# Attention blocks of a hybrid transformer step: transposes, values and scores issued in one run ahead of the block's whole filling work

## The chip, the cores and the metric

The kernel runs on one core of a Trainium2 chip. TensorE (PE) does the matrix products and the transposes and writes only into PSUM, whose eight banks hold 512 columns each here. VectorE (DVE), ScalarE (ACT) and GpSimd (POOL) do the elementwise work; the SyncE queue (SP) issues the transfers. The metric is the device time of one execution in microseconds (us).

## The reference

Two trunk layers over 512 latent and 128 context tokens of width 1024. Cut to what matters here:

```python
h = modulate(rms_norm(x, lw['g_attn']), sh1, sc1)
cb, cc, cv, gq, gk, gv, nq, nk, nv, mq, mkv, mkr, gates = in_project(h, lw['w_in'])
y_conv = short_conv(cb, cc, cv, lw['w_conv'])
y_gqa = banded_window_attention(q_g, k_g, v_g, k_ctx, v_ctx, sink, ATTN_SCALE)      # 8 heads
y_na = neighbourhood_attention(nq, nk, nv, k_ctx, v_ctx, lw['na_rpb'], ATTN_SCALE)  # 4 heads
y_mla = dense_attention(q_mla, [k_lat, k_ctx], [v_lat, v_ctx], MLA_SCALE)           # 4 heads, latent keys
out = merge_branches(gates, y_conv, y_gqa, y_na, y_mla, lw)                         # sigmoid gates, then w_o
x = x + gt1 * out
x = x + gt2 * squared_relu_mlp(modulate(rms_norm(x, lw['g_mlp']), sh2, sc2), lw['w_ff1'], lw['w_ff2'])
```

Context tokens go through the same layers with dense attention among themselves. All data is float32.

## The kernel before, in words

**Products.** A float32 product is made of three products of rounded halves, x and w each being split into a high and a low part. `steps` issues, for one half of the tokens (320 columns) and each of eight slices of the inner dimension, three matmuls (lines 226 to 228) into one PSUM bank and then yields, telling 410 ns as its cost; eight such steps fill a bank. These rows are called dense below, three to a step.

**The attention stage** (`mixers`, once a layer) walks 16 heads: 8 windowed, 4 neighbourhood, 4 with latent keys (`Mla`, heads m0 to m3). A head has five blocks of 128 queries: four latent ones, in two pairs, and one of context tokens. So 80 blocks a layer are worked off by `attend`, whose round i handles two of them at once:

- of block i: `block_T` transposes its probabilities on PE (line 568, up to four per bank), ACT copies the high part out of PSUM (line 571), and `block_lo` on DVE makes the low part (line 575), after which the bank is free;
- of block i+3 (AHEAD is 3): `block_scores` (PE lines 503 to 508, into one of two double banks, then the row minimum on DVE), `block_exp` (ACT, line 548), `block_norm` (POOL, line 553);
- of a finished pair: `values_out`, which is `pair_pv` (PE, line 585, probabilities times values), a copy on ACT (line 589) and the sum into y on DVE (lines 598 to 608).

**The fill.** The layer's projections, convolutions and gates are the other half of the stage. They are generators in one list, FILL: `q1` to `q3`, `c0` to `c3`, `nq`, `nk`, `nv`, `ckv`, `mq`, `kr` and `m0` to `m3`, where None is one gate chunk (16 dense steps) and the number of an entry says how many gate chunks are mixed in between its own steps. `fill(ns)` advances them in the order of the list until their costs have used up ns; a task that waits for a head (`wait`) stops the list for that round. RATE is the ns that a block gets. `block_scores` of a head's first block calls `need`, which runs the list up to the tasks of that head at once, whatever it costs, and takes the cost off the next rounds. `m0` to `m3` (`Mla.prep`) project the queries and keys of one latent head (and at m0 and m2 the values of two).

**Order before.** PE's order is the program's. In a round: transposes, half of the block's fill, scores and exp, the other half (PART is 0.5). The product with the values is put off: inside `steps`, after the third step of a fresh bank (FRESH is 2), or after the exp of a round more than one later.

**Banks.** The stage has four single banks, for transposes, values and fill together, and two double banks for scores. DVE, ACT, POOL and SP are put in order by the compiler's scheduler in this stage.

Of the kernel before, what the change touches and what calls it, by code (L numbers as in the profile page):

```python
# [38 lines left out]
GQ, GK, GV, NQC, NK, NV, MQ, MKV, CONV, MKR = 0, 4, 5, 6, 8, 10, 12, 14, 15, 99  # L39
HEAD, GATE = 100, 200  # L40
# [9 lines left out]
_N0, _KV = [("nk0", (NK,), 0), ("nv0", (NV,), 0)], ("ckv", (MKV,), 0)  # L50
_NQ0, _NQ1, _NK1, _NV1 = ("nq0", (NQC,), 0), ("nq1", (NQC + 1,), 0), ("nk1", (NK + 1,), 0), ("nv1", (NV + 1,), 0)
_MQ, _KR = ("mq", (MQ, MQ + 1), 0), ("kr", (MKR,), 0)
_END = [("m0", (HEAD,), 2), None, ("m1", (HEAD + 1,), 1), ("c1", (CONV + 3,), 0), ("m2", (HEAD + 2,), 2),
        ("c2", (CONV + 5,), 0), ("m3", (HEAD + 3,), 1), ("c3", (CONV + 1,), 0), None]
FILL = ([*_Q, _C0, _Q3, None, _NQ0, *_N0, None, _KV, _NQ1, None, _NK1, _MQ, _NV1, None, _KR, *_END],
        [*_Q, None, _C0, _Q3, None, _NQ0, None, *_N0, None, _KV, None, _NQ1, None, None, _NK1, _MQ, _NV1, None, _KR,
         *_END])
# [2 lines left out]
Y_OF = {0: 0, 1: 2, 2: 6, 3: 8}  # L60
OUT_K, OUT_V = 0, 3

RATE = (3400, 3500)
PREP = (820, 600, 1200)


AHEAD, PART, LAG, FRESH = 3, 0.5, 1, 2

OWN, ROOT, SPREAD = 1, 2, 3
COLS = dict(bmod=0, gattn=48, gmlp=56, wconv=64, sink=70, gq=78, gkv=80, gfin=81, n=89)  # L70
# [10 lines left out]
class Net:  # L81
# [137 lines left out]
    def steps(self, out, w, x, sl, ks=None):  # L219

        nc = self.nc
        (whi, wlo), (xhi, xlo) = w, x
        ks = ks or [(k, k) for k in range(KC)]
        n = len(ks)
        for i, (kw, kx) in enumerate(ks):
            nc.tensor.matmul(out, lhsT=whi[:, kw, :], rhs=xhi[:, kx, sl], start=(i == 0), stop=False)  # L226
            nc.tensor.matmul(out, lhsT=whi[:, kw, :], rhs=xlo[:, kx, sl], start=False, stop=False)  # L227
            nc.tensor.matmul(out, lhsT=wlo[:, kw, :], rhs=xhi[:, kx, sl], start=False, stop=(i == n - 1))  # L228
            if i == FRESH:
                self.values_out()  # L230
            yield 410

    def half(self, w, x, h, ks=None):
# [375 lines left out]

    def values_out(self):  # L610


        if self.pv:
            R, self.pv = self.pv[0], None
            self.pair_pv(R)
            self.pair_out(R)
# [23 lines left out]
    def attend(self, blocks, fill, budget):  # L640

        n = len(blocks)
        for i in range(AHEAD):
            self.block_scores(blocks[i])
            self.block_exp(blocks[i])
            self.block_norm(blocks[i])
            fill(budget(blocks[i]))
        for i in range(n + 1):
            self.round = i
            B = blocks[i] if i < n else None  # L650
            A = blocks[i + AHEAD] if i + AHEAD < n else None
            ns = budget(B or blocks[-1])
            if B:
                self.block_T(B)
            self.drain_pe(one=True)
            fill(ns * PART)
            if A:
                self.block_scores(A)
            if B:
                self.block_lo(B)  # L660
            if A:
                self.block_exp(A)
            if self.pv and self.pv[1] < i:
                self.values_out()
            fill(ns * (1 - PART))
            if A:
                self.block_norm(A)
            self.drain(1300)
            if B and (B["u"] == 1 or B["kind"] == "ctx"):
                self.values_out()  # L670
                self.pv = B["pair"], i + LAG
        self.values_out()

# [11 lines left out]
    def mixers(self, l, first):  # L685
# [6 lines left out]
        with ExitStack() as s:  # L692
# [149 lines left out]
            blocks = [b for H in heads for b in self.blocks(H)]  # L842
            rate = lambda B: RATE[l] * (0.45 if B["kind"] == "ctx" else 1)
            self.attend(blocks, fill, rate)
# [784 lines left out]
```

## Time and profile before

| what | value |
|---|---|
| median of 3 runs | 2368.55 us (2368.54 to 2372.35) |
| the profiled execution | 2371.4 us, of which 2369.6 us from its first to its last instruction |
| PE busy | 2302.6 us, 97% of the span |
| DVE, ACT, POOL busy | 1391.4, 935.3, 418.9 us (59%, 39%, 18%) |
| mean granted clock of PE | 0.991 of full speed |

A busy share of PE says how much of the time some matmul was under way; idle time of the other engines costs nothing by itself. A wait in the profile is the idle time of an engine ahead of an instruction, put down to whatever released that instruction last.

### The profile page before, as it was taken

How to read it: one execution, taken by the hardware profiler on the slowest of the kernel's cores; microseconds unless marked ns; L12 is line 12 of the kernel's file. 1: busy time of each engine (PE TensorE's matmuls, PEld its weight loads, DVE VectorE, ACT ScalarE, POOL GpSimd, SP SyncE). 2: the span in 40 equal slices, each digit the busy share in tenths (PEclk: the TensorE clock that was granted, in tenths of full speed). 3: DMA queues.
4: the chain of work that ended last, by engine and by line, in shares of the span. 5: the costliest groups of instructions: out<-in, count | busy, mean ns of one | idle time of the engine just before them, and what ended most of it. 6: DMA issues, size and time to landing. Idle time of an engine off the chain costs nothing. (4 is left out here: it accounts for less than half of the span.)

```text
span 2369.6 us, 39989 instructions
## 1 busy us (share of the span) xinstructions
PE 2302.6 (97%) x15766; PEld 2245.0 (95%) x15766; DVE 1391.4 (59%) x2812; ACT 935.3 (39%) x1971; POOL 418.9 (18%) x496
## 2 busy tenths in 40 slices
PE   8999999999999999999999999999999999999998
PEld 4998998899999999999999999988999999999998
DVE  5766666557765786877566656655434554343433
ACT  5555555432224332222254555554322344131311
POOL 0333333112231000000123333322113200000001
PEclk9999999999999999999999999999999999999999
DMA  6331321155541344444331323211424312222222
GB/s 241 99 104 63 104 87 66 66 202 167 174 154 61 139 162 151 160 144 159 116 135 66 110 89 103 86 66 56 170 94 134 99 54 72 80 72 78 74 81 72
DMA packets 91371, 261.33 MB, mean 110 GB/s; under 512 B 10416, under 2 KB 29232, under 8 KB 89776
## 3 DMA queue, kind: packets, MB, share of 16 engines
q1 hardware_dynamic: 91184, 258.78, 32.5%
q8 instruction: 124, 2.03, 0.3%
q14 instruction: 63, 0.52, 0.1%
HBM read 231.31 MB, written 21.92 MB: 107 GB/s over the span
## 5 line engine op out<-in xcount | busy, mean ns | idle before, releaser
L226 PE MATMUL pr<-hhi,whiw 128*128 128x320 f32 (+1 forms) x2752 | 867.8, 315 | 12.8 <-DVE y L598 3.0
L228 PE MATMUL pr<-hhi,wlow 128*128 128x320 f32 (+1 forms) x2752 | 852.2, 310 | 3.0 <-DVE wlow L193 2.1
L227 PE MATMUL pr<-hlo,whiw 128*128 128x320 f32 (+1 forms) x2752 | 852.7, 310 | 0.1
L226 PEld LDWEIGHTS pr<-hhi,whiw 128*128 128x128 f32 (+1 forms) x2752 | 516.2, 188 | 18.5 <-issue 5.6
L228 PEld LDWEIGHTS pr<-hhi,wlow 128*128 128x128 f32 (+1 forms) x2752 | 515.2, 187 | 5.8 <-DVE wlow L193 3.5
L227 PEld LDWEIGHTS pr<-hlo,whiw 128*128 128x128 f32 (+1 forms) x2752 | 516.1, 188 | 3.7 <-DVE hlo L1255 2.6
L192 ACT CAST whiw<-raww 128x1024 fp32r<-128x1024 f32 (+2 forms) x170 | 173.5, 1021 | 298.4 <-PE pr L227 269.4
L226 PE MATMUL pr<-hh,whiw 128*128 128x320 f32 x832 | 257.1, 309 | 0.0
L227 PE MATMUL pr<-hl,whiw 128*128 128x320 f32 x832 | 256.9, 309 | 0.0
L228 PE MATMUL pr<-hh,wlow 128*128 128x320 f32 x832 | 256.9, 309 | 0.0
L193 DVE TENSOR_TENSOR wlow<-raww,whiw 128x1024 fp32r<-128x1024 f32 (+2 forms) x170 | 208.2, 1225 | 61.5 <-ACT whiw L192 60.8
L1210 POOL TENSOR_TENSOR sqs<-sqs,sq 128x320 f32<-128x320 f32 x48 | 47.7, 993 | 972.1 <-ACT sq L1208 944.4
L1008 DVE SCALAR_TENSOR_TENSOR x<-pr,mod,x 128x256 f32<-128x256 f32 x320 | 107.7, 379 | 188.8 <-PE pr L228 186.5
L553 POOL TENSOR_SCALAR p<-p,sm 128x512 f32<-128x512 f32 (+3 forms) x160 | 120.9, 756 | 400.2 <-DVE sm L552 357.7
L548 ACT ACTIVATE p<-S,sm 128x641 f32<-128x641 f32 (+6 forms) x160 | 112.1, 701 | 156.8 <-DVE sm L539 80.0
L981 POOL TENSOR_TENSOR acc<-acc,sg 128x320 f32<-128x320 f32 x96 | 100.3, 1060 | 339.3 <-DVE sg L980 339.3
L226 PEld LDWEIGHTS pr<-hh,whiw 128*128 128x128 f32 x832 | 156.4, 188 | 0.0
L227 PEld LDWEIGHTS pr<-hl,whiw 128*128 128x128 f32 x832 | 156.4, 188 | 0.0
L228 PEld LDWEIGHTS pr<-hh,wlow 128*128 128x128 f32 x832 | 156.4, 188 | 0.0
L575 DVE TENSOR_TENSOR pt<-pr,pt 128x512 fp32r<-128x512 f32 (+2 forms) x240 | 118.8, 516 | 54.2 <-ACT pt L571 52.9
L276 DVE SCALAR_TENSOR_TENSOR junk<-wm,cb 128x1024 bf16<-128x1024 f32 x112 | 136.8, 1222 | 2.0
L190 POOL TENSOR_TENSOR wlow<-raww,whiw 128x512 fp32r<-128x512 f32 (+1 forms) x72 | 94.7, 1316 | 190.9 <-ACT whiw L189 179.3
(224 smaller groups left out, 3796.2 us busy)
## 6 DMA issues: line engine op xcount, KB each, us to landing
raww<-in_w SPq DMA_DIRECT2D x128, 512.0 KB, 3.6
wm<-in_wm SPq DMA_DIRECT2D x80, 512.0 KB, 3.5
raww<-in_wg SPq DMA_DIRECT2D x64, 512.0 KB, 3.6
raww<-in_wa SPq DMA_DIRECT2D x42, 512.0 KB, 3.6
gdram<-gt SPq DMA_DIRECT2D x28, 320.0 KB, 2.2
wm<-in_wm SPq DMA_DIRECT2D x8, 1024.0 KB, 14.4
raww<-in_wo SPq DMA_DIRECT2D x16, 512.0 KB, 3.5
kt<-kt SPq DMA_DIRECT2D x24, 224.0 KB, 4.8
```

Source lines behind the costliest of these rows:

```text
L190: e.tensor_tensor(lo[:, c], raw[:, c], _r(hi[:, c]), ALU.subtract)
L192: nc.scalar.copy(hi, raw)
L193: nc.vector.tensor_tensor(lo, raw, _r(hi), ALU.subtract)
L226: nc.tensor.matmul(out, lhsT=whi[:, kw, :], rhs=xhi[:, kx, sl], start=(i == 0), stop=False)
L227: nc.tensor.matmul(out, lhsT=whi[:, kw, :], rhs=xlo[:, kx, sl], start=False, stop=False)
L228: nc.tensor.matmul(out, lhsT=wlo[:, kw, :], rhs=xhi[:, kx, sl], start=False, stop=(i == n - 1))
L276: nc.vector.scalar_tensor_tensor(self.junk, raw, 1.0, self.cb[v], ALU.mult, ALU.mult, accum_out=self.mod[l]["mod"][:, v, i:i + 1])
L548: nc.scalar.activation(p[:, :B["n"]], B["sc"], AF.Exp, bias=sm[:, 0:1], scale=-1.0, accum_out=sm[:, 1:2])
L553: nc.gpsimd.tensor_scalar(p[:, :n], p[:, :n], sm[:, 1:2], 1.0, ALU.mult, ALU.mult)
L575: self.nc.vector.tensor_tensor(lo, src, _r(hi), ALU.subtract)
L981: nc.gpsimd.tensor_tensor(a, a, sg, ALU.add)
L1008: self.nc.vector.scalar_tensor_tensor(x[:, j, o + a:o + b], ps[:, a:b], m[:, v, g0 + j:g0 + j + 1], x[:, j, o + a:o + b], ALU.mult, ALU.add)
```

## The change

Three edits. The round of `attend` is rearranged: transposes of block i, then at once the product with the values of the pair that ended in the round before, then the scores of block i+3; the step of the delayed PE work (`drain_pe`) comes after them, and the whole fill of the block behind that, in one piece. `steps` no longer calls `values_out`. RATE goes from 3400 and 3500 to 3600 and 3700. The end of the fill list has a gate chunk ahead of m0, takes one gate chunk each out of m0 and m2, and has one more at the end.

```diff
-_END = [("m0", (HEAD,), 2), None, ("m1", (HEAD + 1,), 1), ("c1", (CONV + 3,), 0), ("m2", (HEAD + 2,), 2),
-        ("c2", (CONV + 5,), 0), ("m3", (HEAD + 3,), 1), ("c3", (CONV + 1,), 0), None]
+_END = [None, ("m0", (HEAD,), 1), None, ("m1", (HEAD + 1,), 1), ("c1", (CONV + 3,), 0), ("m2", (HEAD + 2,), 1),
+        ("c2", (CONV + 5,), 0), ("m3", (HEAD + 3,), 1), ("c3", (CONV + 1,), 0), None, None]
...
-RATE = (3400, 3500)
+RATE = (3600, 3700)
...
-AHEAD, PART, LAG, FRESH = 3, 0.5, 1, 2
+AHEAD, LAG = 3, 1
...
             nc.tensor.matmul(out, lhsT=wlo[:, kw, :], rhs=xhi[:, kx, sl], start=False, stop=(i == n - 1))
-            if i == FRESH:
-                self.values_out()
             yield 410
...
             if B:
                 self.block_T(B)
-            self.drain_pe(one=True)
-            fill(ns * PART)
+            if self.pv and self.pv[1] <= i:
+                self.values_out()
             if A:
                 self.block_scores(A)
             if B:
                 self.block_lo(B)
             if A:
                 self.block_exp(A)
-            if self.pv and self.pv[1] < i:
-                self.values_out()
-            fill(ns * (1 - PART))
+            self.drain_pe(one=True)
+            fill(ns)
             if A:
                 self.block_norm(A)
             self.drain(1300)
             if B and (B["u"] == 1 or B["kind"] == "ctx"):
-                self.values_out()
+                assert self.pv is None
                 self.pv = B["pair"], i + LAG
```

What moves on PE, at three places. The first is a filled round of the first layer, the third block of the first head. Before, three dense matmuls stand between the transposes (line 568) and the values (line 585), and nine more dense ones follow these rows ahead of the scores:

```order
L568 MATMUL pr_1000<-ident_94,p_835 128x128 x4
L568 MATMUL pr_1006<-ident_94,p_835 128x128
L226 MATMUL pr_986<-hhi_89,whiw_863 128x320
L227 MATMUL pr_986<-hlo_90,whiw_863 128x320
L228 MATMUL pr_986<-hhi_89,wlow_864 128x320
L585 MATMUL pr_1012<-pt_875,vt_688 128x256 x8
L585 MATMUL pr_1012<-pt_875,vt_688 128x128 x2
```

Now transposes (line 565), values (line 582) and scores (lines 500 and 501) follow one another:

```order
L565 MATMUL pr_1006<-ident_94,p_838 128x128 x4
L565 MATMUL pr_1012<-ident_94,p_838 128x128
L582 MATMUL pr_1015<-pt_881,vt_688 128x256 x8
L582 MATMUL pr_1015<-pt_881,vt_688 128x128 x2
L500 MATMUL S2_1029<-kt_600,qt_620 128x256
L501 MATMUL S2_1029<-kt_601,qt_620 128x256
L500 MATMUL S2_1029<-kt_600,qt_620 128x256
L501 MATMUL S2_1029<-kt_601,qt_620 128x256
```

The dense rows between them have gone behind the scores.

The second place is the last latent head (m3) of the first layer: the keys of the head are made by lines 1458 to 1460, `kt_5000` and `kt_5001` being what the scores of its first block read. Before, three dense matmuls lie between the making of the keys and their use:

```order
L1458 MATMUL pr_5105<-kt_2397,whib_4781 64x384
L1459 MATMUL pr_5105<-kt_2398,whib_4781 64x384
L1460 MATMUL pr_5105<-kt_2397,wlob_4782 64x384
L226 MATMUL pr_5120<-hhi_89,whiw_5012 128x320
L227 MATMUL pr_5120<-hlo_90,whiw_5012 128x320
L228 MATMUL pr_5120<-hhi_89,wlow_5013 128x320
L506 MATMUL S2_5133<-kt_5000,qt_4998 128x512
L507 MATMUL S2_5133<-kt_5000,qt_4999 128x512
L508 MATMUL S2_5133<-kt_5001,qt_4998 128x512
```

Now the keys (lines 1453 to 1455) are followed by six dense matmuls and a round of the head before, whose scores read `kt_4442`; the first scores of m3 come behind the last of these rows, after 27 dense matmuls and the next round's transposes and values:

```order
L1454 MATMUL pr_4992<-kt_2326,whib_4668 64x384
L1455 MATMUL pr_4992<-kt_2325,wlob_4669 64x384
...
L565 MATMUL pr_5020<-ident_94,p_4858 128x128 x4
L565 MATMUL pr_5026<-ident_94,p_4858 128x128 x2
L503 MATMUL S2_5030<-kt_4442,qt_4440 128x128
L504 MATMUL S2_5030<-kt_4442,qt_4441 128x128
L505 MATMUL S2_5030<-kt_4443,qt_4440 128x128
```

The third place is the end of the first layer's attention stage. Before, nine dense matmuls stand between the last transpose and the last 14 matmuls with the values (of the last pair and of the context block). Now the last ten instructions of the stage have no dense one among them; the row of line 225 is the next stage's first:

```order
L565 MATMUL pr_5376<-ident_94,p_5240 128x128 x4
L565 MATMUL pr_5382<-ident_94,p_5240 128x128 x2
L582 MATMUL pr_5386<-pt_5256,vt_4635 128x256 x12
L565 MATMUL pr_5404<-ident_94,p_5285 128x128 x4
L565 MATMUL pr_5410<-ident_94,p_5285 128x128 x2
L565 MATMUL pr_5417<-ident_94,p_5348 128x128
L582 MATMUL pr_5420<-pt_5375,vt_4635 128x256 x12
L582 MATMUL pr_5437<-pt_5416,vt_4635 128x128 x2
L225 MATMUL pr_5486<-hhi_89,whiw_5289 128x320
```

Counted over the stage by the order of PE's rows, rounds that hold no dense matmul and none of `prep` are: outside the latent heads 11 before and 12 now in the first layer, 3 before and 5 now in the second; in the latent heads (one just ahead of them taken in) 5 and 7 before, and now only the last two rounds of each layer. The number of PE's instructions is the same.

## Rows read from the trace of the kernel before

**Rows 1.** The page: its first lines, span and PE's busy time.

```profile
span 2369.6 us, 39989 instructions
PE 2302.6 (97%) x15766; PEld 2245.0 (95%) x15766; DVE 1391.4 (59%) x2812; ACT 935.3 (39%) x1971; POOL 418.9 (18%) x496
```

**Rows 2.** Busy time by stretch, both attention stages; last columns granted clock, DMA.

```profile
76.00:180.00 104.00, 102.27 (x734) 100.73 (x734) 70.09 (x168) 56.33 (x140) 34.25 (x40) 1.00 0.31 93
180.00:245.00 65.00, 59.00 (x414) 56.55 (x413) 42.21 (x132) 39.17 (x103) 21.97 (x36) 0.95 0.21 69
245.00:362.00 117.00, 115.22 (x837) 111.32 (x836) 73.73 (x177) 65.44 (x167) 39.34 (x62) 1.00 0.30 92
362.00:452.00 90.00, 83.71 (x564) 78.64 (x563) 56.20 (x109) 46.13 (x110) 26.98 (x28) 0.96 0.18 61
...
1236.00:1370.00 134.00, 129.85 (x938) 128.49 (x937) 88.19 (x205) 72.62 (x183) 42.60 (x48) 1.00 0.31 99
1370.00:1425.00 55.00, 53.06 (x392) 52.10 (x391) 32.49 (x95) 31.64 (x81) 18.56 (x30) 1.00 0.27 92
1425.00:1490.00 65.00, 64.88 (x482) 62.94 (x481) 40.09 (x103) 35.09 (x93) 22.88 (x45) 1.00 0.35 103
1490.00:1640.00 150.00, 141.10 (x955) 133.50 (x954) 93.27 (x194) 78.11 (x192) 45.19 (x48) 0.97 0.19 63
```

**Rows 3.** Waits of PE in the latent heads: total us, times, longest; both layers.

```profile
PE S L508 <- DVE kt L241: 1.6, 1, 1.6
PE pr L568 <- ACT gt L908: 1.3, 1, 1.3
PE pr L1458 <- DVE pt L575: 0.6, 1, 0.6
...
PE S L508 <- DVE kt L241: 2.4, 2, 1.6
PE pr L226 <- ACT gt L908: 1.1, 1, 1.1
PE pr L1458 <- ACT gt L908: 0.3, 1, 0.3
```

**Rows 4.** Timeline of the first layer, m3's first scores: start, us, instruction, [idle before].

```profile
434.99 2.05 DVE L241 TENSOR_TENSOR kt<-kr,kt 32x896 fp32r<-32x896 f32 x1
...
437.08 1.15 DVE L241 TENSOR_TENSOR kt<-pr,kt 64x512 fp32r<-64x512 f32 x2
437.81 0.79 PE L508 MATMUL S<-kt,qt 96*128 96x512 f32 x1 [1.60 <-DVE kt L241]
```

**Rows 5.** Timeline of two filled rounds of the first layer.

```profile
119.10 0.71 PE L568 MATMUL pr<-ident,p 128*128 128x128 f32 x5
...
120.75 0.68 DVE L575 TENSOR_TENSOR pt<-pr,pt 128x512 fp32r<-128x512 f32 x1
...
125.69 1.25 PE L585 MATMUL pr<-pt,vt 128*128 128x256 f32 x10
126.77 0.33 PE L503 MATMUL S<-kt,qt 128*128 128x256 f32 x1
...
127.30 0.31 PE L226 MATMUL pr<-hhi,whiw 128*128 128x320 f32 x1
```

**Rows 6.** Timeline of the second layer: a wait for a bank in a filled round.

```profile
1258.21 0.33 PE L568 MATMUL pr<-ident,p 128*128 128x128 f32 x1 [1.13 <-DVE pt L575]
```

**Rows 7.** Busy time by stretch again: five rounds without fill, and m3's first scores.

```profile
234.00:242.00 8.00, 6.32 (x49) 5.55 (x48) 7.54 (x29) 7.02 (x20) 3.21 (x5) 1.00 0.24 75
434.00:445.00 11.00, 8.57 (x37) 7.20 (x36) 8.45 (x12) 5.84 (x14) 2.24 (x2) 0.69 0.22 79
```

**Rows 8.** Timeline of the second layer, in rounds without fill: the values' first matmul.

```profile
1422.95 0.33 PE L585 MATMUL pr<-pt,vt 128*128 128x128 f32 x1 [0.92 <-DVE y L608]
```

**Rows 9.** Timeline of the first layer, end of the stage.

```profile
465.17 1.71 PE L585 MATMUL pr<-pt,vt 128*128 128x256 f32 x14
...
468.43 0.39 PE L226 MATMUL pr<-hhi,whiw 128*128 128x320 f32 x1 [1.55 <-DVE y L598]
```

## The prediction, made before the changed kernel was run

> **What bounds the kernel now.** First the page: PE is busy for 2302.6 of the 2369.6 us of the span [rows 1], so a change that leaves PE's instructions as they are can only take from the 67 us in which PE idles, or from stretches at the lower clock. Then the busy times by stretch, window less PE's busy time [rows 2]: in the attention stages PE idles 1.7, 6.0, 1.8 and 6.3 us in the first layer and 4.2, 1.9, 0.1 and 8.9 us in the second, 31 us together, to which the granted clock adds a loss in three of the eight windows (0.95, 0.96, 0.97). The windows are, in this order: windowed heads with fill; their last rounds, many without fill; neighbourhood heads with fill; latent heads. The worst are the latent heads: 6.3 of 90 and 8.9 of 150 us idle, against 1.85% in the four windows of filled rounds (7.8 of 420 us).
>
> Then the waits of PE in the latent heads, and the timeline at one of them. The greatest of one kind is that of the scores' third matmul for the low part of the keys, 1.6 us in the first layer and 2.4 us in two waits in the second [rows 3]. The timeline shows why: the head's keys are made by the burst that `need` calls just ahead of the scores, and DVE first splits the rotary part of the keys (2.05 us) and then the products (1.15 us), while PE stands for 1.60 us [rows 4]. The 11 us around it ran at a granted clock of 0.69, so a stretch of it was at 1.2 GHz instead of 2.4 [rows 7]. Behind each burst the fill has a debt and the next rounds go without any, 12 rounds in the latent heads of both layers.
>
> **The change, part by part. The work itself.** PE issues the same instructions. Grouping them saves nothing: ten matmuls with the values take 1.08 us from their first start (125.69) to the first score (126.77), and the four score matmuls 0.53 us more to the next dense one (127.30) [rows 5], whatever stands around them. Cost nothing. So all of the change is in waits.
>
> **Latent heads.** With RATE up and a gate chunk moved, a head's keys are made a head ahead, not in front of their scores, and no round there is without fill but the last two. Now: 6.3 + 8.9 = 15.2 us idle, and for the clock (1 - 0.96) x 90 + (1 - 0.97) x 150 = 8.1 us of lost full-speed time at most; part of it fell into idle time that is counted already, so I take 6, and 21 us in all. After: the share of filled rounds, 1.85% of 240 us, is 4.4 us. To it come the waits that have nothing to do with `need` but with `prep` filling banks faster than ACT and DVE empty them: 1.3 + 0.6 + 1.1 + 0.3 = 3.3 us now [rows 3], for eight heads; since key and value products now stand closer together, I take 5. That leaves 9.4 us, a gain of 21 - 9.4 = 11.6. Bounds: without prep waits the gain is 16.6; with them three times those seen and only the idle counted, 15.2 - 4.4 - 9.9 = 0.9.
>
> **The end of a stage.** Before, dense matmuls lay ahead of the last 14 products with the values, which then ran 1.71 us without a stop [rows 9]. Now nothing covers the last pair. A transpose's low part is ready 120.75 + 0.68 - 119.10 = 2.3 us after the transposes' start [rows 5]; PE has seven transposes to issue meanwhile, at 0.11 us like the other short matmuls some 0.8 us. So it waits 1.5 us there; with 0.1 for a bank, 1.6 a layer, 3.2 us in all. The 1.55 us before the next stage's first matmul, which waits for the last y [rows 9], stays as it is. Bounds: nothing (if ACT and DVE, without fill, are quicker), and 3 a layer if the clock falls too.
>
> **Rounds without fill outside the latent heads.** There are 17 now for 14. In them the values now follow the next block's transposes directly, so between a pair's last transposes and its values PE has only those scores (0.53 us) and up to five transposes (0.55 us) to do: about 1.1 us against the 2.3 us above. The eight pairs so placed would each wait 1.2 us, 9.6 in all. But before, those windows held 6.0 + 1.9 us of idle time too, with waits such as 0.92 us ahead of the values [rows 8], since in five such rounds DVE is busy for 7.54 of 8 us [rows 7]: DVE paces them in either order. A wait at the values largely takes the place of one at the next transposes, and behind a waiting PE stand only scores that are three blocks ahead of need. I take +2, with bounds 0 and +5.
>
> **Filled rounds.** The burst needs banks: two for transposes, one for values, and the fill's own. In the tightest case a fresh fill bank is wanted after the burst and two more dense steps: from the transposes' start 0.55 + 1.08 + 0.53 + 6 x 0.14 = 3.0 us (the window without idle time, 64.88 us for 482 matmuls [rows 2], gives 0.135 over all kinds, and dense ones lie a little above), and the first transposes' bank is free after 2.3 us. That is 0.7 us of slack, once a head by PE's order, so I take nothing on the whole; before there were waits for banks too, such as 1.13 us [rows 6], and they would go with their places. Bounds: -3 (most bank waits gone) and +19 (below). The page Perfetto Trace Analysis of the Trainium skill (Optimization Strategy) speaks against the burst: a gap that repeats on the engine that should be saturated can mean that there is not enough PSUM for the next tile. By it the same gap would come back once in each head; the wait in [rows 6] is of that kind, but there it is not regular.
>
> **Transfers and the other queues.** Tasks of the fill move with their loads and stores by some rounds; the DMA engines are busy for 0.18 to 0.35 of those windows [rows 2] and the loads keep the order of the fill. Cost nothing; if that cover went, a late weight slab would hold PE before a dense matmul, which no row of these windows shows as a large wait.
>
> **The sum.** -11.6 + 3.2 + 2 + 0 = -6.4 us. From the profiled execution, 2371.4 us (span 2369.6 and 1.8 around it), that is 2365.0; it lies 2.85 above the median of the runs, 2368.55, so the forecast for the median is 2362.1, say 2362.
>
> **The rivals.** *Slower: the burst runs out of banks.* If ACT or DVE are late by 1.4 us more than in [rows 5] in an ordinary filled round, as in [rows 6] where DVE was at other work, each of some 27 heads with fill waits 0.7 us: +19, hence 2381. It decides from 0.7 us of lateness on, at 0.24 us a head the gain is gone. For it: four banks for everything, and DVE busy for 62 to 67% of the filled windows [rows 2]. Against it: of the four filled windows the worst idles 4.2 us in 134.
>
> *No net change: the waits of `prep` grow.* Products for keys and values of a head now come back to back and want four banks within about 3 us, while ACT and DVE also split the keys (2.05 us in [rows 4]). With a gain there of 5 us instead of 11.6 and the other terms as they are the time is 2369, with the lower bound of 0.9 it is 2373: say 2369. For it speaks that 3.3 of the 15.2 us in the latent heads are of this kind already.
>
> *More: nothing new shows.* No prep waits, no wait at the stage's end, bank waits gone: -16.6 + 0 + 0 - 3 is 2349; with half of this 2355.
>
> *The clock falls in the burst.* If one stretch at the lower level as in [rows 7], which lost 0.31 x 11 = 3.4 us, came with each of the 27 heads, +90 us. Against it: in five rounds with nothing but transposes, values and scores the granted clock was 1.00 [rows 7], and 1.00 in four of the windows with idle time [rows 2]. The page TensorE: Matmul & The Clock Gate of the Trainium skill (A second HAM failure mode) tells of a kernel in which small idle times between groups that cycle through PSUM banks made the clock swing; the trace here agrees only where PE idled for longer, at m3.
>
> **How the numbers follow.** About 0.2%, 4.7 us, is what a measurement of this kernel can tell from no change, so faster means under 2363.8 and slower over 2373.3. The forecast has a chance of 0.47, the rival that gives more 0.11, no net change 0.25, banks 0.15, the clock 0.02. The forecast's own range is 2357 to 2367, of which a quarter is above 2363.8 and counts as the same: faster 0.35 + 0.11 + some of the others' low ends = 0.50; same 0.33; slower 0.17. The range reaches to the rival that gives more and into the bank rival, 2352 to 2375.
>
> **What the profile after would show.** Right: no wait of the scores for DVE's key split in the latent heads, idle there about 9 us in both layers, no granted clock under 0.98 there; a wait of about 1.5 us at the values in the last rounds of each stage. Wrong: a wait of dense matmuls or transposes for DVE's low part in most heads (banks), or waits at the prep's products that sum to 10 us (no net gain), or a granted clock under 1.00 in the filled windows.

## The result, and the profile after

The changed kernel took 2384.8 us (median of 4 runs, 2382.2 to 2388.7) against 2369.3 us before: a ratio of 1.0064, with a 95% interval of 1.0047 to 1.0082. It is slower by 15 us where 6 us less was forecast. Six more runs beside a later experiment (e15) gave 1.0048 (1.0034 to 1.0062).

The page of the profiled run after (2384.64 us) begins with these lines, to be read against [rows 1]:

```profile
span 2382.8 us, 40003 instructions
...
PE 2309.4 (97%) x15766; PEld 2250.1 (94%) x15766; DVE 1390.3 (58%) x2812; ACT 939.1 (39%) x1971; POOL 419.8 (18%) x496
```

The number of matmuls is the same. Span less PE's busy time was 67.0 us and is 73.4: 6.4 us more idle time. PE's busy time grew by 6.8 us for the same matmuls: some of them ran at the lower clock or came less closely packed.

Where this happened is read from the windows. [rows 2] is cut by time, so here are both kernels cut at the same places of the program: at the scores of the 1st, 23rd, 41st and 58th of a layer's 80 blocks and at the stage's end, to half a microsecond or so. First the kernel before (columns as in [rows 2]: width, busy time of PE, PEld, DVE, ACT and POOL, granted clock, DMA):

```profile
76.00:181.00 105.00, 103.27 (x742) 101.73 (x741) 70.95 (x170) 56.33 (x140) 34.25 (x40) 1.00 0.30 92
181.00:241.00 60.00, 54.00 (x376) 51.56 (x375) 38.07 (x121) 36.85 (x97) 19.73 (x33) 0.94 0.20 65
241.00:326.00 85.00, 83.97 (x612) 80.83 (x611) 55.72 (x139) 47.75 (x123) 31.46 (x53) 1.00 0.34 102
326.00:469.00 143.00, 134.41 (x933) 128.44 (x933) 84.53 (x174) 72.35 (x174) 37.48 (x40) 0.98 0.18 62
1238.00:1348.00 110.00, 106.14 (x763) 105.06 (x764) 73.88 (x170) 58.84 (x146) 36.57 (x41) 1.00 0.26 87
1348.00:1425.00 77.00, 75.06 (x554) 74.07 (x554) 44.87 (x128) 43.47 (x114) 24.46 (x37) 1.00 0.33 107
1425.00:1508.00 83.00, 81.00 (x585) 78.32 (x584) 54.15 (x134) 44.28 (x118) 30.43 (x52) 0.98 0.31 93
1508.00:1655.00 147.00, 138.76 (x953) 131.75 (x952) 85.66 (x175) 74.68 (x179) 37.63 (x41) 0.98 0.18 62
```

The changed kernel, the same heads:

```profile
76.00:187.00 111.00, 106.83 (x751) 104.88 (x752) 72.97 (x173) 59.34 (x146) 35.54 (x42) 0.98 0.28 89
187.00:250.00 63.00, 54.18 (x377) 51.58 (x377) 39.18 (x123) 35.88 (x94) 19.61 (x33) 0.94 0.20 68
250.00:340.00 90.00, 88.87 (x638) 86.10 (x638) 54.50 (x136) 49.38 (x126) 32.26 (x54) 0.98 0.33 98
340.00:475.50 135.50, 128.35 (x893) 121.98 (x892) 81.73 (x168) 69.64 (x167) 37.00 (x39) 0.99 0.17 59
1246.00:1358.00 112.00, 109.86 (x794) 109.37 (x794) 72.57 (x172) 61.15 (x151) 36.82 (x43) 1.00 0.30 96
1358.00:1434.00 76.00, 71.90 (x523) 69.94 (x523) 44.39 (x125) 41.44 (x107) 22.48 (x36) 1.00 0.27 92
1434.00:1529.00 95.00, 91.60 (x659) 88.10 (x659) 60.59 (x143) 52.05 (x133) 34.08 (x55) 0.99 0.32 97
1529.00:1664.70 135.70, 129.16 (x873) 123.32 (x872) 78.22 (x162) 67.71 (x162) 35.03 (x38) 0.96 0.16 56
```

The eight windows together grew from 810.0 to 818.2 us; the other 5 us of the span lie outside the two stages. By kind, idle time and (1 - clock) x width before and after: windows with fill (1st, 3rd, 5th, 7th) 8.6 + 1.7 us and now 10.8 + 5.0; windows with many rounds without fill (2nd, 6th) 7.9 + 3.6 and now 12.9 + 3.8; latent heads (4th, 8th) 16.8 + 5.8 and now 13.7 + 6.8. So the latent heads, for which the change was forecast to give 11.6 us, gave 2, and the rest lost 11. A second profiled execution of the changed kernel (e15), cut at the same scores, gives in the same order 11.4 + 6.4, 13.2 + 1.9 and 13.8 + 4.0 us: the idle times repeat to within 1 us, while the clock's part of a kind differs by 1 to 3 us. By that execution the latent heads gave 5 and the rest lost 11.

What PE waits for has changed its place. These rows of the waits over the whole run (total us, times, longest) are the changed kernel's at the values (line 582) and at the spread of the norm's roots (line 1330):

```profile
PE pr L582 <- DVE pt L572: 4.6, 8, 1.1
PE pr L582 <- ACT gt L903: 4.5, 5, 1.9
PE pr L1330 <- POOL rtykv L1323: 4.2, 1, 4.2
PE pr L582 <- DVE kt L238: 3.5, 2, 1.8
...
PE pr L582 <- ACT st L851: 0.8, 1, 0.8
...
PE pr L582 <- ACT pt L568: 0.5, 2, 0.2
...
PE pr L582 <- ACT st L321: 0.3, 1, 0.3
```

The same rows of the kernel before (values on line 585):

```profile
PE pr L585 <- DVE y L608: 1.7, 2, 0.9
...
PE pr L585 <- ACT st L856: 0.8, 1, 0.8
...
PE pr L585 <- ACT pt L571: 0.7, 1, 0.7
...
PE pr L585 <- ACT p L548: 0.4, 1, 0.4
```

PE waited 3.6 us at the values and now waits 14.2. The scores' wait for the low part of the keys [rows 3] is gone, as forecast.

### The profile page after: what moved, and what is told of

It is laid out like the page before. It is cut to its first block, busy times and chain, and to the rows that moved or that the text cites. A ratio compares the mean times of both kernels' runs of the same rounds, so it can differ in the third digit from the quotient of the medians.

```text
span 2382.8 us, 40003 instructions
## 1 busy us (share of the span) xinstructions
PE 2309.4 (97%) x15766; PEld 2250.1 (94%) x15766; DVE 1390.3 (58%) x2812; ACT 939.1 (39%) x1971; POOL 419.8 (18%) x496
## 5 line engine op out<-in xcount | busy, mean ns | idle before, releaser
L225 PE MATMUL pr<-hhi,whiw 128*128 128x320 f32 (+1 forms) x2752 | 856.0, 311 | 4.8 <-ACT st L321 1.5
L568 ACT CAST pt<-pr 128x512 fp32r<-128x512 f32 (+2 forms) x240 | 100.7, 453 | 83.2 <-PE pr L565 82.1
```

What stands on the lines that cost most here:

```text
L568: nc.scalar.copy(B["split"][-1][0], src)
```

## Two of the new waits, read instruction by instruction

The longest wait at the values, in a filled round of the latent heads of the first layer (timeline of the changed kernel: start, duration, instruction, idle time before it and its releaser):

```profile
367.98 0.30 PE L227 MATMUL pr<-hhi,wlow 128*128 128x320 f32 x1
...
368.83 0.93 PE L565 MATMUL pr<-ident,p 128*128 128x128 f32 x6
...
369.23 0.96 DVE L539 TENSOR_REDUCE sm<-S 128x1 f32<-128x768 f32 x1
370.28 0.90 ACT L545 ACTIVATE p<-S,sm 128x768 f32<-128x768 f32 x1 [1.48 <-POOL wlow L189]
...
371.17 0.43 ACT L903 ACTIVATE gt<-pr 128x320 f32<-128x320 f32 x1
...
371.49 0.57 ACT L237 CAST kt<-pr 64x512 fp32r<-64x512 f32 x1
...
371.65 0.44 PE L582 MATMUL pr<-pt,vt 128*128 128x128 f32 x2 [1.90 <-ACT gt L903]
```

The dense product ends at 368.3. Its bank is emptied by a gate activation on ACT, but that stands in ACT's order behind the exp of the next block, and the exp waits for the row minimum, which DVE ends at 370.19 (the profile names POOL's line 189, which ended 0.01 us later, but the exp reads the minimum). ACT stands idle for 1.48 us with the gate behind the exp. Two banks hold the new transposes, a third the products for the next head's keys, which ACT casts still later (371.49): all four are taken, and the values get none until the gate has been read. The Trainium skill, page Perfetto Trace Analysis (Tensor Engine Instruction (MATMUL, LD_WEIGHTS)), says that ACT is strictly first in, first out; these rows agree: 0.9 us of exp and 1.48 us of idle time ahead of a gate whose input was there.

The second place is in the second layer:

```profile
1584.39 2.00 DVE L238 TENSOR_TENSOR kt<-kr,kt 32x896 fp32r<-32x896 f32 x1
...
1586.42 1.15 DVE L238 TENSOR_TENSOR kt<-pr,kt 64x512 fp32r<-64x512 f32 x2
...
1587.16 0.44 PE L582 MATMUL pr<-pt,vt 128*128 128x128 f32 x2 [1.73 <-DVE kt L238]
```

This is the key split of [rows 4] again: 2.00 us for the rotary part, then 1.15 us for the products. Before, the scores waited 1.60 us for its result; now the scores come much later, but the products' banks are held until the split has read them, and the values, third in line for a bank, wait 1.73 us. The wait was moved, not taken away.

The granted clock of some stretches behind such waits, in the same run:

```profile
102.90:106.30 3.40, 3.40 (x18) 3.40 (x17) 2.90 (x6) 1.15 (x4) 0.69 (x1) 0.51 0.34 99
208.80:212.20 3.40, 3.40 (x18) 3.40 (x17) 2.13 (x8) 0.85 (x2) 0.80 (x1) 0.50 0.00 0
...
372.70:376.00 3.30, 3.30 (x14) 3.01 (x13) 3.24 (x7) 3.18 (x8) 0.66 (x1) 0.50 0.44 169
1587.80:1597.80 10.00, 10.00 (x45) 9.77 (x44) 4.58 (x11) 4.09 (x9) 1.81 (x2) 0.50 0.25 79
```

They are at 1.2 GHz. Two follow the two waits just shown, one the 4.2 us at the spread, one two waits of 0.94 and 0.77 us.

## The experiments

Theory A: the values are the third in a row to want one of four banks, and find none. Rival B: they come too soon after the transposes of their own pair, whose low parts DVE hasn't made. Rival C: the new list and RATE lose the time. Ratios are to the kernel before on the same chip, each of 4 to 12 runs; idle is span less PE busy time of the one profiled run; the clock is the mean granted clock of all runs of the kernel, and lost is (1 - clock) x span, worked out before rounding.

| kernel | ratio (95%) | idle us | clock | lost us |
|---|---|---|---|---|
| before | 1 | 67.0 | 0.991 to 0.992 | 19 to 22 |
| changed | 1.0064 (1.0047 to 1.0082) | 73.4 | 0.989 | 26 |
| changed, again (e15) | 1.0048 (1.0034 to 1.0062) | 72.9 | 0.990 | 24 |
| e1: values apart | 0.9966 (0.9952 to 0.9979) | 67.6 | 0.995 | 13 |
| e2: list alone | 0.9996 (0.9986 to 1.0006) | 71.8 | 0.993 | 16 |
| e3: rearrangement alone | 1.0019 (1.0009 to 1.0030) | 72.1 | 0.993 | 17 |
| e4: delayed step first | 1.0037 (1.0024 to 1.0050) | 72.4 | 0.990 | 23 |
| e6: second bank last | 0.9990 (0.9981 to 0.9999) | 67.5 | 0.993 | 16 |
| e7: apart, old list | 1.0015 (1.0006 to 1.0024) | 68.6 | 0.991 | 21 |
| e8: apart, delayed step first | 0.9981 (0.9969 to 0.9993) | 65.7 | 0.994 | 14 |
| e9: values behind the scores | 0.9998 (0.9986 to 1.0010) | 69.3 | 0.994 | 13 |
| e10: e6, delayed step first | 0.9986 (0.9976 to 0.9997) | 66.5 | 0.993 | 16 |
| e11: e8 and e6 together | 0.9970 (0.9956 to 0.9983) | 64.9 | 0.994 | 14 |
| e12: e1 with the old RATE | 1.0013 (1.0000 to 1.0026) | 69.9 | 0.991 | 20 |
| e13: e1 with the old list's end | 1.0014 (1.0002 to 1.0027) | 72.8 | 0.993 | 18 |
| e14: exp behind the fill | 1.0050 (1.0037 to 1.0062) | 69.9 | 0.988 | 28 |

### The values put back into the fill (e1)

```diff
+            if i == FRESH:
+                self.values_out()
             yield 410
...
-            if self.pv and self.pv[1] <= i:
-                self.values_out()
...
             if A:
                 self.block_exp(A)
+            if self.pv and self.pv[1] < i:
+                self.values_out()
```

> Only the product with the values is taken out of the run of short matmuls again and put off as before (after the third dense step of a fresh bank, or after the exp of a later round); transposes and scores stay together, the fill stays whole, list and RATE stay new. Theory A (the values find no free bank directly behind the transposes) and theory B (the values come too early after their own transposes, ahead of DVE's low parts): PE's waits at the values fall from 14 us to under 5, time 2362 to 2372 us. Theory C (the new list and RATE lose the time): no change, 2380 to 2388 us.

The ratio is 0.9966: with everything else of the change left in, moving the values alone turns 15 us of loss into 8 of gain. This is the largest effect of the study, and it refutes C. The latent heads of this kernel:

```profile
332.00:466.00 134.00, 127.99 (x905) 122.12 (x904) 82.55 (x173) 72.02 (x172) 39.42 (x40) 1.00 0.18 62
1521.00:1652.60 131.60, 125.09 (x884) 119.56 (x883) 80.45 (x171) 70.41 (x169) 35.85 (x39) 1.00 0.19 60
```

They idle for 12.5 us at a clock of 1.00, against 16.8 + 5.8 before: 10 us less. So the latent heads do give about what was forecast for them, when the values don't come in the run. The waits at the values here are 8.9 us, not the few that were expected; they hurt less than their sum says.

### List alone, rearrangement alone (e2, e3)

e2 is the kernel before with the new end of the list and RATE, e3 the changed kernel with the old ones:

```diff
-_END = [("m0", (HEAD,), 2), None, ("m1", (HEAD + 1,), 1), ...
+_END = [None, ("m0", (HEAD,), 1), None, ("m1", (HEAD + 1,), 1), ...
-RATE = (3400, 3500)
+RATE = (3600, 3700)
```

> The kernel before with only the new end of the fill list and the new RATE. Theories A and B: no loss, and the waits of the scores for the keys of their own head go, time 2358 to 2368 us. Theory C: 2378 us or more. That the list gives nothing: 2369 us.

> The changed kernel with the old end of the fill list and the old RATE, so the round's rearrangement alone. Theories A and B: all of the loss and none of the latent heads' gain, 2382 to 2392 us, with PE's waits at the values of 10 us or more. Theory C: 2366 to 2374 us.

The list alone gives nothing (0.9996), a miss for A and B, which expected its gain. The rearrangement alone costs 0.2%, which lies between what A and B expected of it and what C did, so it is a miss for all three. Both together cost 0.5 to 0.6%: the two parts don't add up. In e3 the key waits are where they were before, and few values wait for gates, but more for DVE's low parts (6.4 us, and 4.6 in the changed kernel):

```profile
PE pr L582 <- DVE pt L572: 6.4, 9, 2.1
...
PE S L505 <- DVE kt L238: 3.2, 2, 1.6
...
PE pr L582 <- ACT gt L903: 1.9, 3, 0.8
```

With the new list this 1.9 becomes 4.5 + 3.5 us for gates and key splits, and all waits at the values together go from 11.1 to 14.2. A reading of it, which no run tests by itself: the list has filled the rounds of the latent heads with just those tasks whose banks are emptied late, and the values of the rearranged round stand behind them. In time these waits are the smaller part: from e3 to the changed kernel the idle time grows by about 1 us (72.1 to 73.4 and 72.9), the loss by the clock by 8 to 10 us (17 to 26 and 24).

In e2 the scores' waits for the keys are gone, as they should be, but the values wait longer, 9.9 us in all for 3.6 in the kernel before, most of it in this row:

```profile
PE pr L585 <- DVE pt L575: 7.2, 5, 3.1
```

So there too the wait has come back at another place: the idle time is 4.8 us above that of the kernel before, while the clock loses some 5 us less.

### Breaking up the run of three (e6, e9)

e6 issues the second bank of a block's transposes behind the scores (below; `block_T` then issues one bank a call); e9 leaves the transposes together and puts the two lines with `values_out` behind `block_scores`.

```diff
             if B:
                 self.block_T(B)
             if self.pv and self.pv[1] <= i:
                 self.values_out()
             if A:
                 self.block_scores(A)
+            if B:
+                self.block_T(B, 1)
```

> The changed kernel with the second bank of a block's transposes issued behind the scores, so that the values are the second taker of a bank in the run and not the third; they come no later after their own block's transposes. Theory A: the values' waits for ACT's emptying of a fill bank fall from 6 us to under 2, and the time to 2372 to 2379 us. Theory B: the values' waits stay, 2382 to 2388 us.

> The changed kernel, with the values behind the scores of the run instead of ahead of them (transposes, scores, values, then the fill). Theory A (the values are the third in a row to want a bank): they still come third, only 0.3 to 0.5 us later, so of the waits at the values that go to ACT's gates and to DVE (14.2 us in some 20 waits, the longest 1.9) at most a third goes; ratio to the kernel before 1.0064 less 0.2%, not under 1.004. Theory B (what counts is only the time between a block's own transposes and the values of the pair, whatever bank comes when): the gain is nearly that of the kernel whose second bank of transposes comes behind the scores, so about 0.999 to 1.001.

e6 gives back 0.74% (1.0064 to 0.9990) by the place of the second bank of transposes alone. Its waits at the values are 7.4 us instead of 14.2:

```profile
PE pr L583 <- DVE pt L573: 5.5, 12, 1.1
...
PE pr L583 <- ACT gt L905: 1.4, 2, 0.8
```

Those for ACT fell from 6.1 to 1.9 us, as A forecast, and those for the key split (3.5) are gone. Those for DVE's low parts didn't fall (5.5 for 4.6), so B doesn't explain the gain.

e9 gives back nearly as much (0.9998), where A expected 1.004 or more and B 0.999 to 1.001. B has the ratio right, but not by its own reason: of the 12 to 16 us gained, the waits at the values for DVE's low parts are 1.3 (3.3 for 4.6), and in e1, with the best ratio, these waits are 5.8 us. The waits of e9 show what A had wrong:

```profile
PE pr L565 <- DVE pt L572: 6.4, 10, 2.2
...
PE pr L565 <- ACT gt L903: 4.2, 4, 1.6
...
PE pr L582 <- DVE pt L572: 3.3, 6, 1.0
```

At the values PE waits 6.9 us in all instead of 14.2, but at the transposes 15.1 instead of 9.4: the wait for a bank goes to another taker, and the sum hardly changes (22.0 for 23.6). What changes is the idle time as a whole (69.3 for 73.4 us) and above all the clock, which loses 13 us instead of 26.

So e1, e6 and e9 show, each in its own way, that the place of the values, behind both banks of transposes and ahead of the scores, costs 0.5 to 1%. That the values wait there for banks is read row by row. That the sum of these waits is the time lost is not shown, and e9 speaks against it. One rival is not separated by a run of its own: values ahead of the scores also delay the scores, and with them the exp. Against it speak e6, which puts only one or two transposes (0.11 us each) behind the scores, and e14 below, which delays the exp further at no cost in time.

### Is it ACT's order? (e14, e15)

e14 issues the next block's exp behind the block's fill. PE's order is unchanged; on ACT, gates and key casts now come ahead of the exp in several rounds. e15 is the changed kernel again, on the same chip.

```diff
             if A:
                 self.block_scores(A)
             if B:
                 self.block_lo(B)
-            if A:
-                self.block_exp(A)
             self.drain_pe(one=True)
             fill(ns)
+            if A:
+                self.block_exp(A)
```

> The changed kernel, with the exp of the next block issued behind the block's fill instead of ahead of it. TensorE's order stays as it is; on ACT the evictions of the fill (gates, key casts) come ahead of the exp in several rounds instead of behind it, among them the round in which the values wait 1.9 us for a gate's eviction that stands behind an exp. Theory Q (the values' bank is free late because its eviction queues behind the exp on ACT): the waits of the values for ACT's gates, 4.5 us in the changed kernel, fall under 2, the half-clock stretch behind the longest of them goes too, and the ratio to the kernel before falls by 0.2 to 0.4%, to 1.002 to 1.004. Rival N (four banks are too few for three takers in a row, whatever the order on ACT): the waits move to other releasers, DVE's low parts above all, and the ratio stays at 1.006.

> The changed kernel itself once more, on the chip of these runs, so that the ratios of the kernels with one edit undone can be set against it. If its first result holds: ratio to the kernel before 1.0047 to 1.0082, mean granted clock 0.987 to 0.990.

In e14 the waits of the values for gates are down:

```profile
PE pr L582 <- ACT gt L903: 1.1, 2, 0.8
```

So the reading of the 1.90 us wait was right: with the gate ahead of the exp it is gone. But the time is no shorter (1.0050, against 1.0048 for e15). Part of the wait came back elsewhere: against e15, PE waits 3.4 us less for gates at the values, and for key splits 0.6 us more there (4.1 for 3.5) and 1.7 more at the keys' products (2.0 for 0.3). But other waits fell too: the idle time as a whole is 3.0 us less (69.9 for 72.9), and what levels the time is the clock, which lost 28 us for 24. Theory Q falls as a cause of the time. Rival N has the ratio right, but the moving of the waits, its reason, came only in part; that four banks are short for this run whatever empties them is not shown.

e15 has the same 1.90 us wait as the changed kernel, at 367.79 us of its run. Behind it:

```profile
367.80:376.00 8.20, 8.05 (x54) 7.59 (x55) 6.88 (x15) 6.47 (x15) 2.60 (x2) 1.00 0.42 143
```

The clock stayed at 1.00 there. The same wait is followed by a stretch at 1.2 GHz in one execution and not in another. The reverse is in the record too: the changed kernel's wait of 1.76 us at the values of 1557.83 us is followed by a clock of 1.00, and in e15 by 0.66 over the next 5 us. Only the mean over runs can be compared.

### The delayed step's place (e4, e8, e10)

In the changed kernel, in e1 and in e6:

```diff
             if B:
                 self.block_T(B)
+            self.drain_pe(one=True)
...
-            self.drain_pe(one=True)
             fill(ns)
```

> The changed kernel, with the step of the delayed PE work put back right behind the transposes, where it stood before. Theory D (the place of that step costs time by itself: in the changed kernel one spread matmul waits 4.2 us for POOL's root, because the step now comes after the scores): the 4.2 us wait goes, the ratio to the kernel before falls from 1.0064 by 4.2/2369 = 0.0018 to about 1.0046, and the waits at the values stay as they are, some 14 us. Rival (the spread's wait is only another form of a wait that POOL causes anyway): the ratio stays at 1.006, and another wait for POOL or for the same head's queries stands in its place.

> The kernel with the values apart (new list and RATE), and besides with the step of the delayed PE work put back right behind the transposes. Theory D: the spread's wait of 2.7 us goes, ratio to the kernel before 0.9966 - 2.7/2369 = 0.9955. Rival: another wait takes its place, 0.9966. By either the waits at the values do not grow.

> The changed kernel with the second bank of a block's transposes behind the scores, and the step of the delayed PE work put back right behind the first bank's transposes. Theory D: the spread's wait of 4.2 us goes, and the ratio to the kernel before falls from 0.9990 to 0.9972. Rival: another wait takes its place, 0.999.

The 4.2 us wait at the spread falls to 1.0 us in e4 and 2.1 us in e10, but others take its place (in e4 1.0 us ahead of the root and 1.7 us at the values, for the norm's `st`). The ratios go 1.0064 to 1.0037, 0.9966 to 0.9981 and 0.9990 to 0.9986: no gain of its own that holds in all three. Theory D's ratio is met in e4 alone (1.0037, where it had 1.0046), but by its idle time, 72.4 us for 73.4, only 1 of the 4.2 us is gone.

### Which half of the list, and both repairs (e7, e12, e13, e11)

> The kernel with the values apart (scores right behind the transposes, the whole fill behind them, values inside the fill as before), but with the list and RATE of the kernel before. It tells where the 0.34% of the kernel with the values apart comes from. Theory L (the list gives it, once nothing else waits): without the new list the ratio to the kernel before is 1.000 (0.999 to 1.001), and the waits of the scores for the low part of the keys are back, 1.6 and 2.4 us. Theory G (bringing transposes and scores together ahead of one whole fill gives it, whatever the list): 0.9966, as with the new list. Both in part: 0.998.

> The kernel with the values apart, with the new end of the list but RATE as before (3400 and 3500). With both the ratio to the kernel before is 0.9966, with neither 1.0015. Theory L1 (the place of the gate chunks and of m0 gives the gain): 0.997, and no wait of the scores for the keys' low part. Theory L2 (RATE gives it, since only more fill to a block keeps the list ahead of the heads): 1.001, and the waits for the keys' low part come back, 1.6 us in one head or more of each layer.

> The kernel with the values apart, with the new RATE but the end of the list as before. Theory L2 (RATE gives the gain): 0.997, no wait of the scores for the keys' low part. Theory L1 (the list's end gives it): 1.001, and that wait is back, 1.6 us in each layer. If each gives half, 0.999.

> The kernel with the values apart and the delayed step first, and besides the second bank of a block's transposes behind the scores. Theory A: with the values inside the fill the order of the banks in the run decides nothing more, so the ratio to the kernel before stays at that kernel's 0.998 (0.9966 without the delayed step moved). Rival (a block's second bank of transposes waits by itself, whoever comes behind it): better than 0.996, and fewer waits at the transposes, which sum to 4.7 us in the first layer and 8 us in the second without it.

e7 is e1 with both lines of the list as before, e12 with the old RATE alone, e13 with the old `_END` alone, e11 e1 with the edits of e8 and e6. With the values apart, neither half of the list (e7) gives 1.0015, either one alone 1.0013 and 1.0014, both 0.9966. So bringing transposes and scores together gains nothing, and the 0.5% comes from the list's end and RATE together; both theories of e12 and e13 missed. With one of them the waits of the scores for keys stay (1.5 us in e12, 2.8 in e13, 3.2 in e7); with both they are gone. e11 is no better than e1 (0.9970), as A expected. Its waits at the transposes fell from 14.7 us in e8 to 8.7, as the rival had it, but its idle time only by 0.8 us (65.7 to 64.9).

## Why the prediction was wrong

**The work itself** and **transfers**, costed at nothing: nothing in the rows speaks against either; PE's matmuls are as many as before. Of the 13.2 us by which the profiled run is longer, 6.4 are idle time of PE, and the rest is the same matmuls under way for longer.

**Filled rounds** is the step that failed, in these words: "in the tightest case a fresh fill bank is wanted after the burst and two more dense steps", with 0.7 us of slack, "so I take nothing on the whole". The tightest case is an earlier one: the values themselves, directly behind two banks of transposes, while the fill's last bank still waits for its eviction. The slack there was never computed, though its parts were at hand: two of the four banks are held by the new transposes for 2.3 us [rows 5], and the values come 0.9 us after the first of them (371.65 - 1.90 - 368.83), so they depend on the fill's last banks being emptied within that 0.9 us. In the windows this term is 5.5 us instead of 0 (2.2 idle, 3.3 clock; in e15 2.8 and 4.7), in the latent heads it took back most of their gain, and e1 puts the values' place at 19 to 23 us (0.9966 against 1.0048 and 1.0064). The rival that named banks had the right resource and sign, but the wrong taker. That its 2381 us come near the measured time is in part luck: it is made of 27 equal waits of 0.7 us, where the rows show 14 us at the values in some 20 unequal ones, and the clock. One sum of another rival is off: half of the -19.6 us of the rival that gives more is 2359, not 2355, which lies midway between 2349 and the forecast.

**Latent heads**, -11.6 us: -2 and -5 in the changed kernel's two profiled executions, -10 in e1, and 0.5% of the run between e7 and e1. The mechanism was right and nearly the size; what was missed is that the key split's delay stays with whoever wants the next bank.

**Rounds without fill**, +2 us: +5.2 in the windows (+3.6 in e15); 4.2 us of waiting, in both, is the single wait at the spread, where the edit moved the delayed step behind the values and scores. Without it the term was about right; e8 and e10 show that its loss is not one that a better place gives back.

**The end of a stage**, +3.2 us: about -1. The last rows of the first layer's stage, against [rows 9]:

```profile
472.35 0.84 PE L565 MATMUL pr<-ident,p 128*128 128x128 f32 x3 [0.79 <-DVE pt L572]
...
473.35 2.21 PE L582 MATMUL pr<-pt,vt 128*128 128x256 f32 x14 [0.16 <-DVE pt L572]
...
475.39 0.36 PE L225 MATMUL pr<-hhi,whiw 128*128 128x320 f32 x1
```

There are waits of 0.79 and 0.16 us (in the second layer 0.43, 0.16 and 0.15), but the next stage's first matmul doesn't wait for y any more, which was 1.55 us (1.22 in the second layer) and had been taken to stay.

**The clock** entered the sum only where idle time was to go (6 us, in the latent heads), and beside it as a remote rival of a fall in every head. What the runs show lies between: it loses 23 to 28 us in the kernels with the new list and the values behind both banks of transposes and ahead of the scores (changed, e15, e4, e14), 13 to 14 in e1, e8, e9 and e11. The step that failed here is the reason given against that rival, a granted clock of 1.00 in five rounds without fill and lower ones only at m3. The trace of the kernel before has another stretch among the rounds without fill, columns as in [rows 2]:

```profile
199.00:212.00 13.00, 10.41 (x68) 9.53 (x67) 8.71 (x31) 7.60 (x22) 6.92 (x17) 0.87 0.25 77
```

Part of it, from 201.2 to 205 us, ran at a mean clock of 0.55, behind a wait of 0.81 us, and so did 188.0 to 191.6 us (0.54) behind waits of 0.76 and 0.97 us. Waits of under 1 us went ahead of the lower clock before the change too. The page TensorE: Matmul & The Clock Gate of the Trainium skill (A second HAM failure mode), which the prediction weighed and set aside, tells of a kernel whose clock swings with small idle times between groups that cycle through PSUM banks; the trace agrees at 372.7 us and not at the same wait in e15.

**The signs** that the prediction listed: the scores' wait for the key split is gone, as it said. Idle time in the latent heads is 13.7 us where it said about 9, a clock of 0.96 is there where it said none under 0.98, and the values in the last rounds of a stage wait 0.16 us (0.31 in the second layer) where it said 1.5. Of the signs of being wrong, a granted clock under 1.00 in the filled windows came (0.98, 0.98 and 0.99).

What stays open: why some waits of 1 to 2 us are followed by the lower clock and others are not, as the transposes' 2.15 us at 1259 us of e9 (clock 1.00 behind it); and with it the larger part of the loss, of which the runs show the place and not the mechanism. Open too are why in e2 the values wait longer for DVE, and 5 of the 13 us between the profiled runs, which lie outside the attention stages. The number of banks was not varied in any run.

## What to carry to other kernels

When work is brought together on one engine, count the buffers that the group takes in a row and ask of each one when its last reader is done, in that reader's own queue, not only of the buffer wanted behind the group. Work between takers of the same banks can hide their waits; here, when one taker was moved, waits came back at the next one (e9: 7.3 us less at the values, 5.7 more at the transposes). Edits of a schedule are to be timed in all their combinations: here the new list gave nothing in the old order, 0.5% with the values apart, and cost 0.3 to 0.45% in the rearranged round.

## What was not expected of the hardware

Across these kernels PE's idle time differs by 8.5 us (64.9 to 73.4) and the loss by the granted clock by 15 us (13 to 28): by these figures, the idle times being of one execution each, the clock carries more of the differences than the waits do. And removing a wait of 1.9 us, with its neighbours 3.4 us in all, changed nothing that could be measured in the time (e14).
